# One more seven-product pair in each of the last two up-projection chunks

## The chip, the cores and the metric

The kernel runs on one core of a Trainium2 chip. The metric is the device time of one execution in microseconds (us); several executions are timed and their median is given. One further execution is recorded by the profiler, and it is from that one that all durations of single instructions come. The engines are TensorE (PE, with its weight loads as PEld), VectorE (DVE), ScalarE (ACT), GpSimd (POOL) and SyncE (SP). SP and POOL start almost all transfers; a transfer that adds to what lies at its destination (`accum_op`) is started from POOL here.

## The reference, cut to what matters

One decoder layer for 256 tokens of width 2048, in float32. The change lies in the last block, a feed-forward layer of width 8192:

```
D_MODEL = 2048; SEQ = 256; D_FF = 4 * D_MODEL

h    = _rmsnorm(x, norm_attn_pre)
proj = h @ w_in
...                                   # two kinds of attention, 8 heads each
x = x + _rmsnorm(mixed @ w_out, norm_attn_post)

h = _rmsnorm(x, norm_mlp_pre)
u = jnp.square(jax.nn.relu(h @ w_up))             # 256 x 2048 @ 2048 x 8192
x = x + _rmsnorm(u @ w_down, norm_mlp_post)       # 256 x 8192 @ 8192 x 2048
```

## The kernel before

**Products.** A float32 product is made of three TensorE passes: each operand is split into a high part (rounded by ACT, line 307 or 311) and a low part (the rest, by DVE, line 308 or 312), and the passes are high by high, high by low, low by high (`three`, and the loop at line 297). A pass takes 128 contraction rows, 128 tokens and 512 columns.

**The up projection.** `w_up` is worked on in eight chunks of 1024 columns (`NUP`, chunk index `j` from 0 to 7). A chunk's contraction has 16 blocks of 128 rows. `UP_STEPS[j]` lists a chunk's steps in the order in which they run:

- `("k", k)`: one block of 128 rows the plain way, two token halves by two column halves by three passes, so 12 matmuls.
- `("w", kp)` and `("p", kp)`: a pair, the blocks 2kp and 2kp+1 together, in Winograd's form of Strassen's method. The eight block products of the pair become seven, so 21 matmuls in place of 24 (`seven_products`). It needs four *left* sums of the activations `hT` (made once for each pair by `left_sums`, at the start of the phase) and sums `t` and `u` of the weights. In a `w` pair DVE makes `t` and `u` out of the two raw blocks (`seven`, lines 360 to 365). In a `p` pair they were made in HBM before, by transfers that add (`prepare`, `prepare_all`, tiles `sums`), and are loaded.

Before the change chunk 0 has no pairs. Chunks 1 to 5 have four, `p0`, `w1`, `p2`, `w3`, and eight plain blocks: 8 x 12 + 4 x 21 = 180 matmuls. Chunks 6 and 7 have three, `w0`, `w1`, `w2`, and ten plain blocks: 10 x 12 + 3 x 21 = 183.

The left sums of pairs 0 to 2 lie in tile `st` for the whole phase. Those of pair 3 lie in `st2`, which has the buffer that chunk 5's result `uT10` takes over; from then on they are gone.

**Partial results.** The seven products of a chunk's pairs add up in the chunk's four accumulators and in four more PSUM banks `m1`, `m5`, `m6`, `m7`. After the last pair, `close` puts these together into tile `c` (one ACT copy, line 1073, and four DVE operations, line 1076), and `up_evac` adds `c` to each accumulator (line 970), applies the rectifier and has the result transposed (`rt`) into `uT`.

**Order of the work.** The program order is written out by a small planner. `Flow` holds a clock that each matmul moves on by `MM` (0.2158 us, the planner's own figure); side jobs are generators that yield the time until their next step, and `flow.pump` issues those whose time has come. `Weights` runs ahead of TensorE: `get(i)` for a weight tile emits everything up to tile i+6 (`W_AHEAD`), which is the load into one of five `raw` buffers on SP (line 189) and the split into one of eight `hi`/`lo` pairs. Each engine works through its own instructions in program order, and so do SP and POOL with the transfers that they start: one that waits holds up those behind it.

**What `prepare` issues for one pair**, beginning at a planner time: two plain transfers on SP (lines 593 and 594: block 2kp into `t`, and the right half of block 2kp+1 twice into `u`), `D_PREP[2]` later three adds on POOL (lines 596 to 598, 256 KB each), and `D_PREP[2]` later one add of `t`'s left half to both halves of `u` (line 600, 512 KB). `prepare_all` begins at planner time 50 (`D_PREP[0]`) and goes through ten pairs, 24 us apart.

**How a pair's weights come in.** A `p` pair of chunks 1 to 4 loads `t` and `u` with one POOL transfer into tile `tu` (line 434), one of chunk 5 with two SP loads into `raw` (`j < 5` in the planning loop). A `w` pair loads its two blocks with POOL into tile `ab` (line 378), ahead of time; in chunk 7 the pairs `w1` and `w2` load theirs into two `raw` buffers instead (`raw_w`, in `seven_up`), at the place of their sums.

## Time and profile before

| | |
|---|---|
| median of 3 runs | 1049.08 us (1048.65 to 1049.19) |
| the profiled execution | 1049.02 us, of which its span is 1047.2 us |
| granted TensorE clock, mean | 0.998 |
| HBM read, written | 244.18 MB, 39.32 MB |

The span runs from the first to the last instruction that the profile shows; the 1.8 us beside it lie around it. TensorE's matmuls overlap, so the time that each is recorded with (about 0.39 us) is longer than the distance from one to the next. The chunks of the up projection can be told apart in the chain of work by the transposes `rt` of the chunk before, which stand at the beginning of each. A wait shown for an engine names what ended it.

### The profile page before, as it was taken

How to read it: one execution, taken by the hardware profiler on the slowest of the kernel's cores; microseconds unless marked ns; L12 is line 12 of the kernel's file. 1: busy time of each engine (PE TensorE's matmuls, PEld its weight loads, DVE VectorE, ACT ScalarE, POOL GpSimd, SP SyncE). 2: the span in 40 equal slices, each digit the busy share in tenths (PEclk: the TensorE clock that was granted, in tenths of full speed). 3: DMA queues.
4: the chain of work that ended last, by engine and by line, in shares of the span. 5: the costliest groups of instructions: out<-in, count | busy, mean ns of one | idle time of the engine just before them, and what ended most of it. 6: DMA issues, size and time to landing. Idle time of an engine off the chain costs nothing.

```text
span 1047.2 us, 13576 instructions
## 1 busy us (share of the span) xinstructions
PE 1036.6 (99%) x4844; PEld 863.3 (82%) x4844; DVE 809.0 (77%) x1080; ACT 633.5 (60%) x848; POOL 100.0 (10%) x157
## 2 busy tenths in 40 slices
PE   9999999999999999999999999999999999999996
PEld 6888889888888888888888888888888888888885
DVE  6676536567547669988889798887899988989995
ACT  6675536565545566766766666666567564766662
POOL 0011111112001010010100000000000001122100
PEclk9999999999999999999999999999999999999999
DMA  9999879699878295857766666469779767788952
GB/s 291 376 300 277 227 203 318 203 252 302 234 215 263 90 356 178 290 201 231 267 209 237 210 213 206 149 219 325 248 273 309 268 228 258 267 302 311 377 192 84
DMA packets 93140, 260.81 MB, mean 249 GB/s; under 512 B 8720, under 2 KB 12816, under 8 KB 91664
## 3 DMA queue, kind: packets, MB, share of 16 engines
q1 hardware_dynamic: 71056, 190.09, 52.6%
q0 software_dynamic: 21152, 68.69, 23.2%
q10 hardware_dynamic: 864, 1.16, 0.3%
q8 instruction: 38, 0.62, 0.2%
q14 instruction: 30, 0.25, 0.1%
HBM read 244.18 MB, written 39.32 MB: 271 GB/s over the span
## 4 chain that ended last, share of the span: by engine, by line
PE 97%; DVE 1%; DMA 1%; ACT 0%; issue 0%; POOL 0%; DVEq 0%; ACTq 0%
PE y L297 26%; PE acc_u L297 24%; PE acc_o L297 8%; PE m L297 7%; PE md L297 5%; PE acc_v L297 4%; PE acc_qk L297 4%; PE acc_ckv L297 2%; PE acc_q L297 2%; PE acc_ukv L297 2%; PE acc_cq L297 2%; PE acc_k L297 2%; PE acc_uq L297 2%; PE rt L301 1%; PE y L1221 1%; PE sc_b L297 1%
## 5 line engine op out<-in xcount | busy, mean ns | idle before, releaser
L308 DVE TENSOR_TENSOR lo<-raw,hi 128x1024 fp32r<-128x1024 f32 (+3 forms) x241 | 269.8, 1137 | 93.0 <-ACT hi L307 92.2
L307 ACT ACTIVATE hi<-raw 128x1024 fp32r<-128x1024 f32 (+3 forms) x241 | 234.8, 988 | 92.8 <-PE y L297 20.3
L297 PE MATMUL y<-hi,uhi 128*128 128x512 f32 x376 | 146.7, 390 | 0.0
L297 PE MATMUL y<-hi,ulo 128*128 128x512 f32 x376 | 146.4, 389 | 0.0
L297 PE MATMUL y<-lo,uhi 128*128 128x512 f32 x376 | 146.3, 389 | 0.0
L297 PE MATMUL acc_u<-hi,hT_hi 128*128 128x512 f32 x356 | 141.7, 398 | 0.0
L297 PE MATMUL acc_u<-hi,hT_lo 128*128 128x512 f32 x356 | 139.2, 391 | 0.4 <-DVE hT_lo L308 0.4
L297 PE MATMUL acc_u<-lo,hT_hi 128*128 128x512 f32 x356 | 138.8, 390 | 0.0
L312 DVE SCALAR_TENSOR_TENSOR lo<-raw,gcol,hi 128x1024 fp32r<-128x1024 f32 x72 | 90.7, 1280 | 15.9 <-ACT hi L311 15.6
L311 ACT ACTIVATE hi<-raw,gcol 128x1024 fp32r<-128x1024 f32 x72 | 81.7, 1149 | 19.1 <-DMA raw<-in_w_up 11.9
L297 PEld LDWEIGHTS y<-hi,ulo 128*128 128x128 f32 x376 | 70.6, 188 | 14.6
L297 PEld LDWEIGHTS y<-hi,uhi 128*128 128x128 f32 x376 | 70.6, 188 | 14.5
L297 PEld LDWEIGHTS y<-lo,uhi 128*128 128x128 f32 x376 | 70.6, 188 | 14.5
L297 PEld LDWEIGHTS acc_u<-hi,hT_lo 128*128 128x128 f32 x356 | 66.8, 188 | 15.0 <-DVE hT_lo L308 0.9
L297 PEld LDWEIGHTS acc_u<-lo,hT_hi 128*128 128x128 f32 x356 | 67.0, 188 | 13.0
L297 PEld LDWEIGHTS acc_u<-hi,hT_hi 128*128 128x128 f32 x356 | 66.9, 188 | 12.8
L297 PE MATMUL m<-hi,st 128*128 128x512 f32 x156 | 56.5, 389 | 0.0
L297 PE MATMUL acc_o<-hi,mixT_hi 128*128 128x512 f32 x128 | 51.8, 405 | 0.0
L308 DVE TENSOR_TENSOR lo<-st_down,hi 128x1024 fp32r<-128x1024 f32 x40 | 48.0, 1220 | 4.0 <-ACT hi L307 3.8
L297 PE MATMUL acc_o<-hi,mixT_lo 128*128 128x512 f32 x128 | 50.2, 392 | 0.0
L297 PE MATMUL acc_o<-lo,mixT_hi 128*128 128x512 f32 x128 | 50.0, 391 | 0.0
L307 ACT ACTIVATE hi<-st_down 128x1024 fp32r<-128x1024 f32 x40 | 42.1, 1052 | 11.1 <-PE y L297 9.5
(337 smaller groups left out, 2039.9 us busy)
## 6 DMA issues: line engine op xcount, KB each, us to landing
raw<-in_w_down SPq DMA_DIRECT2D x88, 512.0 KB, 6.2
raw<-in_w_up SPq DMA_DIRECT2D x86, 512.0 KB, 4.5
raw<-in_w_in SPq DMA_DIRECT2D x55, 512.0 KB, 6.7
raw<-in_w_out SPq DMA_DIRECT2D x32, 512.0 KB, 7.3
ab<-in_w_up POOLq DMA_DIRECT2D x28, 512.0 KB, 5.0
sums<-in_w_up SPq DMA_DIRECT2D x20, 512.0 KB, 6.9
ab_down<-in_w_down POOLq DMA_DIRECT2D x20, 512.0 KB, 6.5
tu<-sums POOLq DMA_DIRECT2D x8, 1024.0 KB, 5.2
```

Of the source, the lines that this page charges most:

```text
L297: nc.tensor.matmul(out, a, b, start=start, stop=stop)
L301: nc.tensor.transpose(out, a, ident)
L307: nc.scalar.activation(hi, src, AF.Copy)
L308: nc.vector.tensor_tensor(out=lo, in0=src, in1=hi.bitcast(F32), op=OP.subtract)
L311: nc.scalar.activation(hi, src, AF.Copy, scale=g)
L312: nc.vector.scalar_tensor_tensor(out=lo, in0=src, scalar=g, in1=hi.bitcast(F32), op0=OP.mult, op1=OP.subtract)
L1221: nc.tensor.matmul(out, a[x], w[z], start=False, stop=(x, z) == (1, 0), skip_group_check=True)
```

## The change

Chunks 6 and 7 get the step list of chunks 1 to 5: `p0`, `w1`, `p2`, `w3` and eight plain blocks in place of `w0`, `w1`, `w2` and ten plain blocks. What goes with it:

- `PREP` has fourteen pairs where it had ten. `prepare_all` goes through the first twelve, at 22.6 us apart with 11.3 us between the steps where it was 24 and 12.
- The last two, both of chunk 7, are prepared by two runs of `prepare` with `slow` = 10.0, started in chunk 2 and in chunk 4: the same bytes, with the last add cut into two, one transfer every 10 us, seven for a pair.
- `left_sums` writes pair 3's left sums to HBM (`st_kept`, 512 KB on SP) 8 us after it has made them. In chunks 6 and 7, at the fourth step, they are loaded into the buffer of tile `c`, which then lies idle until `close`; before `close` a new `c` is taken from that buffer, which is free once the last pair's products have been read.
- The `p` pairs of chunks 6 and 7 load their sums as those of chunk 5 do, by SP into `raw`. In chunk 7 no pair uses `ab` any more.
- The pause between `up_evac`'s add and its rectifier is 2.4 us where it was 1.8 in chunk 1.

```diff
 UP_STEPS = {0: [("k", k) for k in range(KD)]}
-for _j in range(1, 6):
+for _j in range(1, NUP):
     UP_STEPS[_j] = steps_of("k8 k9 k10 k11 p0 k12 w1 k13 p2 w3 k14 k15")
-for _j in range(6, NUP):
-    UP_STEPS[_j] = steps_of("k6 k7 k8 k9 k10 w0 k11 k12 w1 k13 w2 k14 k15")
...
-D_PREP = (50.0, 24.0, 12.0)
+D_PREP = (50.0, 22.6, 11.3)
...
-                ts, after = plan_seven(*seven_up(j, k), after, soon=j < NUP - 1 or k == 0)
+                ts, after = plan_seven(*seven_up(j, k), after, soon=j < NUP - 1)
...
-    def prepare(j, kp):
+    def prepare(j, kp, slow=0):
...
+        def add(out, src):
+            nc.gpsimd.dma_start(out=out, in_=src, accum_op=OP.add)
+
         nc.sync.dma_start(out=t, in_=a)
+        if slow:
+            yield slow
         nc.sync.dma_start(out=u.rearrange("p (k n) -> p k n", k=2), in_=twice(b[:, H:]))
-        yield D_PREP[2]
-        nc.gpsimd.dma_start(out=t[:, :H], in_=a[:, H:], accum_op=OP.add)
-        nc.gpsimd.dma_start(out=t[:, H:], in_=b[:, H:], accum_op=OP.add)
-        nc.gpsimd.dma_start(out=u[:, H:], in_=b[:, :H], accum_op=OP.add)
-        yield D_PREP[2]
-        nc.gpsimd.dma_start(out=u.rearrange("p (k n) -> p k n", k=2), in_=twice(t[:, :H]), accum_op=OP.add)
+        yield slow or D_PREP[2]
+        for out, src in ((t[:, :H], a[:, H:]), (t[:, H:], b[:, H:]), (u[:, H:], b[:, :H])):
+            add(out, src)
+            if slow:
+                yield slow
+        if not slow:
+            yield D_PREP[2]
+            add(u.rearrange("p (k n) -> p k n", k=2), twice(t[:, :H]))
+            return
+        for k in range(2):
+            add(u[:, k * H:(k + 1) * H], t[:, :H])
+            yield slow
...
-        for jk in PREP:
+        for jk in PREP[:-2]:
...
-            yield 1.8 if j < 10 else 2.4
+            yield 1.8 if 4 <= j < 10 else 2.4
...
+    st_kept = dram.tile([P, CW], F32, name="st_kept")
+
+    def new_c(name, dt=F32):
+        return late["up"].tile([P, 2 * CW], dt, tag="c", bufs=1, name=name)
...
+        if kp == 3:
+            yield 8.0
+            nc.sync.dma_start(out=st_kept, in_=sp.bitcast(F32))
...
+            if (j, t, b) in ((2, 2, 0), (4, 2, 0)):
+                flow.start(prepare(*PREP[j // 2 - 3], 10.0))
+            if j > 5 and (t, b) == (3, 0):
+                late["st2"] = new_c(f"st2_{j}", F32R)
+                nc.sync.dma_start(out=late["st2"][:, :CW].bitcast(F32), in_=st_kept)
+                sums[3] = parts_of(late["st2"])
...
             if last:
+                if j > 5:
+                    late["c"] = new_c(f"c_{j}")
                 more = close(closing(), m)
```

More of the change, by code (lines that the diff above doesn't have):

```diff
@@ L1024, in layer, with parts_of @@
     sums = []
+    st_kept = dram.tile([P, CW], F32, name="st_kept")
+    def new_c(name, dt=F32):
+        return late["up"].tile([P, 2 * CW], dt, tag="c", bufs=1, name=name)
+    def parts_of(st):
+        return [[st[:, w * 512 + i * P:w * 512 + (i + 1) * P] for w in range(2)] for i in range(4)]
     def left_sums(kp):
@@ L1101, in layer @@
                 late["st"] = late["up"].tile([P, 3 * CW], F32R, tag="st", bufs=1, name="st")
-                for n in ("ab", "c"):
-                    late[n] = late["up"].tile([P, 2 * CW], F32, name=n)
+                late["ab"], late["c"] = late["up"].tile([P, 2 * CW], F32, name="ab"), new_c("c")
                 late["st2"] = late["up"].tile([P, CW], F32R, tag="uT10", bufs=1, name="st2")
```

## The prediction

> **What bounds the kernel now.** I read the page first, then TensorE's waits, then the chain of waits in order of time.
>
> ```profile
> span 1047.2 us, 13576 instructions
> PE 1036.6 (99%) x4844; PEld 863.3 (82%) x4844; DVE 809.0 (77%) x1080; ACT 633.5 (60%) x848; POOL 100.0 (10%) x157
> ```
> ```profile
> PE warm L538 <- DVE zero L535: 1.2, 1, 1.2
> PE acc_qk L297 <- ACT hi L307: 0.8, 1, 0.8
> PE acc_u L297 <- DVE hT_lo L308: 0.4, 1, 0.4
> PE qrt L301 <- DVE qT L805: 0.2, 1, 0.2
> ```
>
> TensorE is the bound from end to end. Its waits for other engines come to 2.6 us, none of them in chunks 1 to 7. So there is no stall to remove: the change gains what it takes out of TensorE's stream, and loses whatever stalls it makes.
>
> What is a matmul worth? The chain shows stretches that nothing interrupts, and the first full stretch behind the first transposes of each chunk:
>
> ```profile
> 482.28 8.16 PE acc_u L297 x36
> ...
> 533.59 2.09 PE acc_u L297 x9
> ...
> 576.32 2.09 PE acc_u L297 x9
> ...
> 619.80 2.08 PE acc_u L297 x9
> ...
> 663.24 2.10 PE acc_u L297 x9
> ...
> 706.64 2.08 PE y L297 x9
> ```
>
> 36 matmuls in 8.16 us are 0.2267 us each. From 533.59 to 576.32, chunk 4 with its 180 matmuls takes 42.73 us. From 619.80 to 663.24, chunk 6 takes 43.44 us, and from 663.24 to 706.64 chunk 7 takes 43.40 us, with 183 matmuls and the same sixteen transposes.
>
> **The change part by part.**
>
> *The products.* In each of chunks 6 and 7, two plain blocks (24 matmuls) become one pair (21). That is 6 matmuls fewer, 6 x 0.2267 = 1.36 us. The chunks say the same in another way: (43.44 - 42.73) + (43.40 - 42.73) = 1.38 us. I take **-1.4 us**, all of it on the path, since TensorE waits for nothing there.
>
> *DVE in chunks 6 and 7.* Two `w` pairs take the place of three, so DVE makes one set of sums fewer and has two plain blocks fewer to split, against one pair more to split. DVE is off the path; I count nothing.
>
> *Twelve early pairs in place of ten.* Pairs 1 to 10 move up by 1.4 us each. Pairs 11 and 12 (of chunk 6) are new; worked out from the delays and the planner's 0.216 us a matmul, they fall into the output projection, about 300 to 350 us.
>
> ```profile
> sums<-in_w_up SPq DMA_DIRECT2D x20, 512.0 KB, 6.9
> sums<-in_w_up POOLq DMA_DIRECT2D x30, 256.0 KB, 8.9
> sums<-sums POOLq DMA_DIRECT2D x10, 512.0 KB, 9.2
> ```
> ```profile
> 300.00:350.00 50.00, 50.00 (x222) 41.06 (x221) 29.63 (x41) 24.38 (x40) 3.37 (x3) 1.00 0.71 231
> ```
>
> A pair is two plain transfers, three small adds and one large one, 2.25 MB written. Two pairs are 4.5 MB, at this window's 231 GB/s 19.5 us of transfers, against 0.29 x 50 = 14.5 us in which the transfer engines stand idle there, and a TensorE that is busy for 50.00 of 50 us. The cost lies between 0 and the 5 us that do not fit; I take 0, because weights are made several tiles ahead and a delay first eats that lead. POOL matters as well, since it computes the norms' powers that the next phase waits for:
>
> ```profile
> 321.80 1.20 POOL L600 DMA_DIRECT2D sums<-sums  x1
> 349.10 0.56 POOL L518 TENSOR_TENSOR rstd_post<-t_post,neg_half 128x1 f32<-128x1 f32 x1 [26.10 <-DVE t_post L517]
> 362.42 0.55 POOL L518 TENSOR_TENSOR rstd_post<-t_post,neg_half 128x1 f32<-128x1 f32 x1 [12.76 <-DVE t_post L517]
> ```
>
> Pair 12's small adds come some 4 us of planner time ahead of the first `rstd_post`, so they should go out near 330 us and have landed before 349. Its last add stands between the two `rstd_post`: it goes out at about 350 and takes 1.2 us of POOL, with 12.76 us to spare. Cost 0. If the small adds slip behind the first `rstd_post`, the last one waits 8.9 us for them and still ends at about 362.
>
> *Two pairs by small transfers in chunks 2 to 5.* Seven transfers each, 10 us of planner time apart, two on SP and five on POOL. POOL has `tu` and `ab` loads there that wait long for DVE, and the adds queue among them:
>
> ```profile
> 459.52 0.54 POOL L378 DMA_DIRECT2D ab<-in_w_up  x1 [3.05 <-DVE lo L308]
> 470.07 0.54 POOL L434 DMA_DIRECT2D tu<-sums  x1 [10.01 <-DVE lo L308]
> 494.83 0.54 POOL L434 DMA_DIRECT2D tu<-sums  x1 [22.48 <-DVE lo L308]
> ```
>
> By the planner's times the first add falls between these first two rows, the second before the third row, and so on: nearly all fall into POOL's gaps of 10 and 22 us and cost it about 1 us of issue each. One can push an `ab` load back by 1 us. I take 0, that load's lead being several us.
>
> The Trainium skill (DMA: Bandwidth & Descriptors, "Rules for kernel authors") advises the opposite, to coalesce small transfers into large ones. The rows bear this out for the single transfer: 256 KB of adds land in 8.9 us, 512 KB in 9.2 us, so cutting the last add in two buys a second landing. Going by the rule, a pair here costs one landing more; the sum stays the same, since these sums are needed only in chunk 7.
>
> *Pair 3's left sums, out.* `st_kept` goes on SP 8 us of planner time after its sums are made. SP runs ahead of DVE, so it will wait there, with a `raw` load behind it:
>
> ```profile
> 403.47 0.33 SPq L189 DMA_DIRECT2D raw<-in_w_up  x1
> ```
> ```profile
> 417.09 0.68 DVE L1042 TENSOR_TENSOR st<-c,st 128x512 fp32r<-128x512 f32 x1
> 422.90 1.82 DVE L308 TENSOR_TENSOR lo<-raw,hi 128x512 fp32r<-128x512 f32 x2
> 427.22 2.35 DVE L308 TENSOR_TENSOR lo<-tu,hi 128x1024 fp32r<-128x1024 f32 x2
> ```
> ```profile
> 420.83 1.57 ACT L307 ACTIVATE hi<-raw 128x512 fp32r<-128x512 f32 x2
> ```
> ```profile
> 431.82 0.68 PE m L297 x3
> ```
>
> By the planner's times `st_kept` comes just ahead of the load at 403.47. `st` is complete only at 417.09 + 0.68 = 417.8, so that load moves from 403.5 to about 418.3, and its split on ACT, the second of the two at 420.83 (from 421.35), is next. Loads of this stretch and of the whole run land as follows:
>
> ```profile
> DMA to landing us min/median/max: 3.5/4.5/5.5
> ```
> ```profile
> DMA to landing us min/median/max: 2.7/5.5/15.9
> ```
>
> At 4.5 us it lands at 422.8, 1.4 us late for ACT; DVE, which has about 1.1 us of room there, is 0.4 us late. At 15.9 us it lands at 434.2, and DVE is 11.8 us late. The smallest lead behind it is that of the first `tu` tile: ready at 428.4, used at 431.8 (the row of `m`), 3.4 us. So the cost to TensorE is between 0 and 8.4 us, with 0 up to a landing of 7.5 us. I take 0, by the nearest row, the stretch's own largest of 5.5 us.
>
> *Pair 3's left sums, back.* `c` carries them from the fourth step to the last pair, and `close` must wait until the last pair's products are read.
>
> ```profile
> L1073 ACT ACTIVATE c<-m x7: 575/577/581, 440.0 to 697.0; 128x512 f32<-128x512 f32 x7
> ```
>
> It does so already: in chunk 1 the pairs' last matmul begins near 439 and the copy at 440.0. What is queued behind it on ACT are splits for the next chunk. Cost 0. Two loads of 512 KB on SP wait for the `c` of the chunk before, which is read by then. The longer pause in chunk 1 delays transposes, not TensorE: 0.
>
> *Loads in chunk 7.* Five `raw` buffers serve 8 plain blocks, 2 x 4 loads of `p` and 2 x 2 of `w`, 20 loads, where there were 10 + 4. In a `p` beside a `w`, `u` takes the buffer of five loads before. DVE then has 0.69 + 1.23 us of splits and four sums to do meanwhile:
>
> ```profile
> 680.60 0.68 DVE L363 TENSOR_TENSOR t<-raw_w 128x512 f32<-128x512 f32 x1
> ...
> 682.52 0.69 DVE L365 TENSOR_TENSOR u<-u,raw_w 128x512 f32<-128x512 f32 x1
> ...
> 688.53 1.22 DVE L308 TENSOR_TENSOR lo<-t,hi 128x1024 fp32r<-128x1024 f32 x1
> ```
> ```profile
> 696.00 1.36 PE m L297 x6
> ```
> ```profile
> DMA to landing us min/median/max: 3.5/4.4/7.8
> ```
>
> The sums run from 680.60 to 683.2, so about 4.5 us lie between. A load needs 4.4 us and ACT's split 1.05 (the `raw` splits above): 1 us of idle DVE, twice in the chunk. At 7.8 us it is 4.4 us, twice. The last `w` tile is ready at 689.75 and used at 696.00, a lead of 6.2 us. So 0 by the median, up to 2.6 us by the maximum; I take 0. In chunk 6 the loads are those of chunk 5, which stalls nowhere.
>
> **Sum.** 1047.2 - 1.4 = 1045.8 us of span; with the 1.8 us around it 1047.6. The profiled execution (1049.02) lies 0.06 us below the median of the runs, so **1047.7 us**.
>
> **The rivals.**
>
> 1. *SP stands behind `st_kept`.* For it: 14 us of blocked SP in the stretch with the smallest leads. Against: 0 cost up to a landing of 7.5 us. At 9.2 us, the largest adding transfer's median, DVE is 5.1 us late and TensorE 1.7 us: 1049.4 us, the gain just gone.
> 2. *Chunk 7 starves for `raw` buffers, and the kernel is slower.* It decides once 2 x (landing - 3.4) passes 6.2, a landing of 6.5 us. With the 9.2 us of the adding transfers TensorE loses 11.6 - 6.2 = 5.4 us: 1053.1 us. Against: the 4.4 us median.
> 3. *A matmul is worth what it is recorded with.*
>
> ```profile
> L297 PE MATMUL m<-hi,st 128*128 128x512 f32 x156 | 56.5, 389 | 0.0
> ```
>
> 6 x 0.389 = 2.3 us would give 1046.7. Against: 36 in 8.16 us.
>
> 4. *The transfers share one pool.* The row of 300:350 leaves up to 5 us that do not fit; if half of it gets through to TensorE, 1047.7 + 2.5 = 1050.2 us. The Trainium skill (DMA: Bandwidth & Descriptors, "Issuing engines are not separate DMA queues") says that transfers from all queues run on the same sixteen engines and interleave, so moving work to POOL would spare SP's loads nothing; no row here separates the two.
>
> **How the numbers follow.** Forecast 0.70, within 1047.3 to 1048.1. Rival 1: 0.11. Rival 2: 0.07. Rival 3: 0.03. Rival 4: 0.09. About 0.2% (2.1 us) is what a measurement of this kernel can tell from no change; the forecast lies within it. Faster is rival 3, 0.03. Slower is rival 2 and the far end of rivals 1 and 4: 0.07 + 0.02 = 0.09. The rest, 0.88, is the same. The range reaches from 1047.0 to 1049.6, over the forecast and rival 1, and leaves out rivals 2, 3 and 4, 0.19.
>
> **What would show it.** Chunks 6 and 7 at 42.7 us each in the chain. TensorE's waits still without a row in chunks 1 to 7. SP's load behind `st_kept` at 418, ACT idle about 1 us for it near 421.4. A wait of PE for `lo` near 432 or in chunk 7 is rival 1 or 2; one for `hi` or `hT_lo` before 380 is rival 4. A chunk that gets shorter by more than 0.7 us would make the worth of a matmul wrong.

## The result: slower by 0.8%, and the profile after

The changed kernel takes 1057.65 us (median of 6 runs, 1054.79 to 1060.76) against 1049.13 us before, a ratio of 1.008 with a 95% interval of 1.0066 to 1.0093. The profiled execution is the shortest of the six, 1054.79 us with a span of 1053.0 us, 5.8 us more than before.

From the page of the changed kernel: its span, and busy time with its share of the span and number of instructions for each engine.

```profile
span 1053.0 us, 13632 instructions
...
PE 1037.0 (98%) x4838; PEld 861.8 (82%) x4838; DVE 808.2 (77%) x1078; ACT 636.9 (60%) x852; POOL 113.9 (11%) x171
```

TensorE's waits in the changed kernel (what it waited for: us in total, times, longest):

```profile
PE rt L299 <- ACT r L983: 2.1, 4, 0.7
PE acc_u L295 <- DVE c L1095: 1.7, 2, 1.4
PE acc_u L295 <- ACT hT_hi L305: 1.7, 1, 1.7
...
PE m L295 <- DVE lo L306: 0.8, 1, 0.8
```

The six matmuls are gone (4844 recorded before, 4838 now). Four waits of the up projection that the kernel before did not have are there in their place. Where they fall is seen by cutting the up projection at the first transposes `rt` of each chunk. Starts of instructions, worked out from each trace, in us; "chunk 0" runs from the last `w_out` matmul to the transposes that stand at the start of chunk 1, "rest" from the transposes behind chunk 7 to the end. Differences in the text are taken before rounding:

| kernel | before chunk 0 | chunk 0 | 1 | 2 | 3 to 5 | 6 | 7 | rest | span |
|---|---|---|---|---|---|---|---|---|---|
| before | 354.5 | 49.4 | 43.6 | 42.8 | 128.9 | 43.4 | 43.5 | 341.2 | 1047.2 |
| changed | 353.9 | 51.5 | 48.3 | 42.1 | 128.9 | 42.7 | 44.2 | 341.6 | 1053.0 |
| changed, second profile | 354.2 | 51.2 | 48.3 | 42.1 | 128.9 | 42.7 | 44.6 | 341.6 | 1053.6 |

So the time went to three places: **chunk 0** (+2.0 us), **chunk 1** (+4.7, of which chunk 2 gives 0.7 back, so +4.0 together), and **chunk 7**, which should have shortened by 0.7 like chunk 6 and is 0.7 longer. Chunk 6 has its gain. The second profile, of a run described below, has the same three places.

**Chunk 0.** The changed kernel's timeline on POOL, on SP's queue and on ScalarE (start, duration, engine, line, operation; in brackets how long the engine sat idle before it, and what ended that):

```profile
338.84 3.02 POOL L592 DMA_DIRECT2D sums<-in_w_up  x3
348.48 0.57 POOL L516 TENSOR_TENSOR rstd_post<-t_post,neg_half 128x1 f32<-128x1 f32 x1 [6.62 <-DVE t_post L515]
353.42 1.20 POOL L592 DMA_DIRECT2D sums<-sums  x1 [4.37 <-issue]
361.82 0.57 POOL L516 TENSOR_TENSOR rstd_post<-t_post,neg_half 128x1 f32<-128x1 f32 x1 [7.20 <-DVE t_post L515]
```
```profile
355.83 0.38 SPq L187 DMA_DIRECT2D raw<-in_w_up  x1
```
```profile
364.37 1.15 ACT L309 ACTIVATE hi<-raw,gcol 128x1024 fp32r<-128x1024 f32 x1 [3.89 <-DMA raw<-in_w_up]
...
366.80 1.07 ACT L305 ACTIVATE hT_hi<-ht 128x512 fp32r<-128x512 f32 x2
```

POOL runs in the order that the prediction gave: pair 12's three small adds ahead of the first `rstd_post`, its last add between the two, both `rstd_post` on time. The times are later than forecast: the small adds go out at 338.8 in place of about 330, the last add at 353.4 in place of 350. What is late is a transfer of another queue: the raw `w_up` load that SP issues at 355.83, beside that last add. And ScalarE works in order: while it waits 3.89 us for this load (1.00 us in the kernel before), `hT_hi`, for which TensorE waits, stands behind the split.

**Chunk 1.** The chain of waits of the changed kernel, in order of time (start, us, what held the chain):

```profile
421.21 8.99 DMA ab<-in_w_up
...
430.32 1.24 DVE t L358
...
440.51 4.46 DMA raw<-in_w_up
...
445.07 1.16 ACT hi L309
...
452.84 0.70 ACT r L983
453.58 0.66 PE rt L299 x4
```

On DVE, the first load that SP had held back, and then that `ab` load:

```profile
425.72 1.23 DVE L306 TENSOR_TENSOR lo<-raw,hi 128x1024 fp32r<-128x1024 f32 x1 [0.74 <-ACT hi L305]
430.32 1.23 DVE L358 TENSOR_TENSOR t<-ab 128x1024 f32<-128x1024 f32 x1 [3.38 <-DMA ab<-in_w_up]
```

The first link is again a transfer, the second of POOL's two `ab` loads for pair `w3`, at 9.0 us. In the kernel before, the same two loads (issued between 418 and 421 us; KB each, median us from issue to landing) took 4.0:

```profile
ab<-in_w_up POOLq DMA_DIRECT2D x2, 512.0 KB, 4.0
```

DVE waits 3.38 us for it, makes `w3`'s sums late, frees the `raw` buffers late, a load that waits for a buffer lands late, and the copy `c<-m` of `close`, with all that follows from it, is late.

**Chunk 7.** SP's queue and ScalarE in the changed kernel:

```profile
657.52 1.67 SPq L187 DMA_DIRECT2D raw_w<-in_w_up  x2
662.71 0.33 SPq L187 DMA_DIRECT2D raw<-sums  x1
```
```profile
668.34 1.06 ACT L305 ACTIVATE hi<-raw 128x1024 fp32r<-128x1024 f32 x1 [3.19 <-DMA raw<-sums]
...
669.79 0.68 ACT L983 ACTIVATE r<-acc_u,rstd_pre 128x512 f32<-128x512 f32 x1
```

Two of the five `raw` buffers hold `w1`'s raw blocks ahead of time, the second load of `p0`'s sums (the first goes out at 656.3) finds a buffer only at 662.7, and again it is ScalarE's order that carries it to TensorE: `r`, which the transposes need, stands behind the split. TensorE waits 0.6 us for it here, and another 0.7 us for `r` at the end of the chunk.

### The profile page after: what moved, and what is told of

The parts are those of the page before. It is cut to its first block, busy times and chain, and to the rows that moved or that the text cites. A ratio compares the mean times of both kernels' runs of the same rounds, so it can differ in the third digit from the quotient of the medians.

```text
span 1053.0 us, 13632 instructions
## 1 busy us (share of the span) xinstructions
PE 1037.0 (98%) x4838; PEld 861.8 (82%) x4838; DVE 808.2 (77%) x1078; ACT 636.9 (60%) x852; POOL 113.9 (11%) x171
## 4 chain that ended last, share of the span: by engine, by line
PE 85%; issue 6%; DMA 4%; DVE 3%; ACT 1%; POOL 0%; DVEq 0%; ACTq 0%; POOLq 0%
PE y L295 25%; PE acc_u L295 14%; PE acc_o L295 8%; PE m L295 5%; PE md L295 5%; PE acc_v L295 4%; PE acc_qk L295 4%; PE acc_ckv L295 2%; PE acc_ukv L295 2%; PE acc_q L295 2%; PE acc_cq L295 2%; PE acc_k L295 2%; PE acc_uq L295 2%; DVE lo L306 2%; DMA raw<-in_w_up 1%
## 5 line engine op out<-in xcount | busy, mean ns | idle before, releaser
L306 DVE TENSOR_TENSOR lo<-raw,hi 128x1024 fp32r<-128x1024 f32 (+3 forms) x253 | 282.6, 1133 | 102.6 <-ACT hi L305 101.6
L305 ACT ACTIVATE hi<-raw 128x1024 fp32r<-128x1024 f32 (+3 forms) x253 | 245.9, 985 | 116.5 <-DMA raw<-in_w_in 26.0
L295 PE MATMUL acc_u<-hi,hT_hi 128*128 128x512 f32 x344 | 137.3, 399 | 3.3 <-DVE c L1095 1.7
L295 PE MATMUL acc_u<-hi,hT_lo 128*128 128x512 f32 x344 | 134.5, 391 | 0.5 <-DVE hT_lo L306 0.5
L295 PE MATMUL acc_u<-lo,hT_hi 128*128 128x512 f32 x344 | 134.0, 390 | 0.0
L295 PEld LDWEIGHTS acc_u<-hi,hT_hi 128*128 128x128 f32 x344 | 64.6, 188 | 16.6 <-DVE c L1095 2.5
L295 PEld LDWEIGHTS acc_u<-hi,hT_lo 128*128 128x128 f32 x344 | 64.6, 188 | 14.8 <-DVE hT_lo L306 0.9
L295 PEld LDWEIGHTS acc_u<-lo,hT_hi 128*128 128x128 f32 x344 | 64.7, 188 | 12.3
L295 PE MATMUL m<-hi,st 128*128 128x512 f32 x168 | 60.8, 389 | 0.0
L305 ACT ACTIVATE hi<-st_down 128x1024 fp32r<-128x1024 f32 x40 | 42.1, 1053 | 11.3 <-PE y L295 9.8
```

Source lines behind the costliest of these rows:

```text
L295: nc.tensor.matmul(out, a, b, start=start, stop=stop)
L305: nc.scalar.activation(hi, src, AF.Copy)
L306: nc.vector.tensor_tensor(out=lo, in0=src, in1=hi.bitcast(F32), op=OP.subtract)
```

## The experiments

The theory is those three places, named **A** (pair 12's last add beside chunk 0's raw load), **B** (SP blocked by `st_kept`; the loads held back go out together and slow the `ab` loads) and **C** (chunk 7's `raw` buffers). All edits below are against the changed kernel or, where it says so, the kernel before. What each run measured stands in one table at the end of this section.

**The changed kernel again.**

> The changed kernel once more, for a second profile of it. If the three losses read from its first profile are what it always has, the stretch around chunk 0 is again about 2 us longer than before, that of chunk 1 about 4 us and that of chunk 7 about 1.5 us; what a slower execution (up to 1060.8) has on top should show as further waits of TensorE in the opening or in chunks 0 and 1.

It had 1055.41 us (1051.99 to 1059.33), and the stretches shown above as the second profile: the three places are not of one execution.

**A, undone.** Pair 12 is taken out of the opening and prepared by a third slow run:

```diff
-        for jk in PREP[:-2]:
+        for jk in PREP[:-3]:
...
-            if (j, t, b) in ((2, 2, 0), (4, 2, 0)):
-                flow.start(prepare(*PREP[j // 2 - 3], 10.0))
+            if j in (2, 3, 4) and (t, b) == (2, 0):
+                flow.start(prepare(*PREP[j - 5], 10.0))
```

> The changed kernel with the twelfth early pair taken out of the opening: it is prepared by small transfers in chunks 2 to 4, and chunk 7's two pairs begin in chunks 3 and 4. Theory: the twelfth pair's last adding transfer (issued at 353.4, landed at 360.6) made the weight load issued at 355.8 land at 364.4, 8.6 us instead of 5.7; ACT stood 3.9 us for it ahead of the splits of hT, and TensorE lost 2.0 us in chunk 0. Then the time from the last w_out matmul to chunk 0's first transpose (49.4 us before, 51.4 with the change) comes back to 49.4 and the span falls by 2.0 to about 1051. Rival: POOL's order (the norm's power behind the adds) is what is late; then the wait for hT stays in part, because pair 11 still has its adds there.

Chunk 0 is back at 49.5 us. What lies before chunk 0 took until 356.3 us in this profile, 2.4 longer, so the span hardly moved and missed the 1051 us expected.

**A, alone.** The kernel before, with the two pairs of chunk 6 prepared in the opening at the change's pace, their sums unused:

```diff
-D_PREP = (50.0, 24.0, 12.0)
+D_PREP = (50.0, 22.6, 11.3)
+MORE = [(6, 0), (6, 2)]
...
-        for jk in PREP:
+        for jk in PREP + MORE:
```

> The kernel before, with the eleventh and twelfth pair prepared in the opening at the change's pace (22.6/11.3) and nothing else; their sums are not used. Theory A (the twelfth pair's last adds beside chunk 0's raw load): the stretch from the opening's end to chunk 0's first transposes goes from 49.4 to 51 to 52.5 us, with the scalar engine idle for that raw load near 360 to 364; time 1050.5 to 1053, and a spread between executions of 3 us or more, as in the changed kernel. Rival (the loss needs the rest of the change): 49.4 and 1049.2.

And the same without pair 12's last add (`if (j, kp) != (6, 2)` ahead of it):

> As the run with the two further pairs alone in the kernel before, but without pair 12's last add (512 KB, out about 353 us), whose sums are not used. Theory (that one transfer, beside the raw load of about 356, is what the opening loses): from the opening's end to chunk 0's first transposes 49.4 to 49.8 us where it was 52.9, the raw load lands within 6 us, the time 1049 to 1050. Rival (pair 12's small adds and the rest of its traffic do it as well): 51 us or more, 1051 or more.

Groups of transfers between 353 and 366 us (KB each, median us from issue to landing), with the last add and without it:

```profile
sums<-sums POOLq DMA_DIRECT2D x1, 512.0 KB, 9.8
raw<-in_w_up SPq DMA_DIRECT2D x1, 512.0 KB, 8.6
```
```profile
raw<-in_w_up SPq DMA_DIRECT2D x1, 512.0 KB, 5.7
```

One transfer of 512 KB on POOL's queue makes SP's raw load land in 8.6 us in place of 5.7. Chunk 0 goes from 49.4 to 52.8 us with it (a little past what was expected) and is 49.5 without it. In place, A is shown: it is that add, not the twelfth pair's bytes as a whole. In time the second run missed its expectation by a little: 1050.33 us, with an interval that holds no change (0.9997 to 1.0016); chunk 1 was 1.1 us longer in its profile, and 1.0 us in that of the run with the add, so that part is not the last add's.

**A, by placing.** Pair 12 stays in the opening at a pace of 21.4/10.7 (and B and C are undone as shown further down), so that its last add goes out earlier:

```diff
-D_PREP = (50.0, 22.6, 11.3)
+D_PREP = (50.0, 21.4, 10.7)
```

> Pair 12 back in the opening, but at a pace of 21.4/10.7 us instead of 22.6/11.3, so that its last add goes out about 14 us earlier in the order of work than in the changed kernel, ahead of the last half of the opening, and not beside the raw w_up load that is issued near 356; the write of pair 3's left sums a tile later and chunk 7's loads a tile later as in the run before; the two slow pairs in chunks 2 and 4 as in the change. Theory A (pair 12's last add slows that raw load, and the scalar engine's splits queue behind it): the opening's end to chunk 0's first transposes comes back to 49.4 us from 51.4, the raw load lands within 6 us of its issue, and the time is 1048.0 to 1050. Rival (twelve pairs are too many for the opening wherever they stand): 51 or more, or w_out ends later than 356.5; time 1051 or more.

Chunk 0 49.4 us, the raw load at 5.6 us, 1048.85 us. The last add now goes out at 338.0 in place of 353.4, and the same bytes cost nothing there that chunk 0 or the opening shows.

**B, undone.** The write of pair 3's left sums a good deal later, when SP no longer overtakes DVE's sums:

```diff
-            yield 8.0
+            yield 40.0
             nc.sync.dma_start(out=st_kept, in_=sp.bitcast(F32))
```

> The changed kernel with one number altered: pair 3's left sums are written to HBM 40 us of planner time after they are made instead of 8, so that SP no longer stands waiting for them in chunk 1. Theory: in chunk 1 SP stood 14 us behind that transfer and then let it and the held-back weight loads go together with POOL's two ab loads, which landed at 427.6 and 430.2 instead of 422.6 and 423.9; DVE stood idle 3.4 us for the second and TensorE lost about 4 us between chunk 1's first transpose and chunk 2's. Then that stretch (43.6 us before, 48.3 us with the change) comes back to about 44.2 us and the profiled span falls from 1053.0 to about 1049. Rival: the longer pause before chunk 1's rectifier, or the 512 KB themselves, cost the time; then the stretch stays near 48 us.

Chunk 1 comes down from 48.3 to 44.3 us. The span, 1051.0, is 2 us over the expected one; chunk 0 took 52.5 us in this profile. With A undone as well:

> Both of the two other alterations together. If the two losses are separate, they add: chunk 0 as before, chunk 1 about 0.6 us longer than before, and what is left of the change is 6 matmuls fewer (1.4 us) against the waits at the ends of chunks 6 and 7 (about 1.9 us): a span near 1047.5, a time near 1049.3, and the wide spread of the single times gone. If the losses feed each other, one of the two alterations gives most of it and the sum falls short.

Both places are back (49.4 and 44.0), but the time is 1051.97 us, not 1049.3, and the spread (4 us) is not gone: C remains, and the opening ended at 356.5 us in this profile.

**B, alone.** The kernel before, with the write and nothing that reads it:

```diff
+        if kp == 3:
+            yield 8.0
+            nc.sync.dma_start(out=st_kept, in_=sp.bitcast(F32))
```

> The kernel before, with the write of pair 3's left sums to HBM added at the change's place (8.0) and nothing else; what is written is not read. Theory B (the blocked SP queue and its burst are what chunk 1 lost, whatever the pairs do): the stretch of chunk 1 goes from 43.56 to 46.5 to 48.5 us, the time from 1049.1 to 1052 to 1054. Rival (it takes the extra slow transfers or the twelfth pair as well): 43.5 to 44.5 us and 1049 to 1050.

It is 1053.13 us, a ratio of 1.0039 (1.0026 to 1.0052), with 4.0 us in chunk 1. The write alone thus costs nearly three times what the products bring. Is it the 512 KB or the wait? The same, with two columns (1 KB) in place of all:

```diff
-            nc.sync.dma_start(out=st_kept, in_=sp.bitcast(F32))
+            nc.sync.dma_start(out=st_kept[:, :2], in_=sp[:, CW - 2:].bitcast(F32))
```

> The kernel before, with a write at the same place and with the same wait as in the run of the write alone, but of two columns of the left sums (1 KB) in place of all 1024 (512 KB). SP is blocked as long; only the bytes are gone. Theory (SP's loads, held back and let go together, slow the ab loads): the stretch of chunk 1 stays at 46.5 to 47.6 us, the time at 1052 to 1053. Rival (the 512 KB written beside them are what takes the time): 43.5 to 44.5 us, 1049 to 1050. In between, both have a part.

Transfers between 418 and 432 us (total, then groups with KB each and median us to landing) in the kernel before, with the whole write, and with 1 KB:

```profile
DMA packets 871, 3.24 MB, mean 231 GB/s; under 512 B 98, under 2 KB 98, under 8 KB 855
...
ab<-in_w_up POOLq DMA_DIRECT2D x4, 512.0 KB, 4.9
raw<-in_w_up SPq DMA_DIRECT2D x3, 512.0 KB, 4.5
```
```profile
DMA packets 1297, 4.73 MB, mean 338 GB/s; under 512 B 144, under 2 KB 144, under 8 KB 1296
...
raw<-in_w_up SPq DMA_DIRECT2D x6, 512.0 KB, 7.3
ab<-in_w_up POOLq DMA_DIRECT2D x2, 512.0 KB, 8.2
st_kept<-st SPq DMA_DIRECT2D x1, 512.0 KB, 3.0
```
```profile
DMA packets 1297, 4.20 MB, mean 300 GB/s; under 512 B 272, under 2 KB 272, under 8 KB 1296
...
raw<-in_w_up SPq DMA_DIRECT2D x6, 512.0 KB, 6.4
ab<-in_w_up POOLq DMA_DIRECT2D x2, 512.0 KB, 6.5
```

With 1 KB, SP stands as long and six raw loads fall into the window in place of three; chunk 1 is 46.9 us. `w3`'s second `ab` load took 4.1 us in the kernel before, 7.7 with 1 KB and 8.9 with the whole write; chunks 1 and 2 together are longer by 3.3 and 4.0 us. So most of the 4.0 us is there without the write's bytes. The 0.7 between the two runs is of one profile each, and their times (ratios 1.0039 and 1.0026) do not tell them apart.

Does it matter which loads are held back? The write at 13 in place of 8 has one more load ahead of it (A undone here):

> As the run with both parts undone (pair 12 late, the write of the left sums late), but that write's place set between the change's and the late one: 13 instead of 8 or 40. The load that stood right behind the write in the change now stands ahead of it; the write still blocks SP until pair 3's sums are done, near 418, and loads behind it go out together. Theory (the loads that were held back go out in a burst and slow the ab loads on POOL's queue, and pair 0's left sums of chunk 1 come late): chunk 1 stays long, 46 to 48.5 us from its first transposes to those of chunk 2 (44.0 with the write late), with the ab transfers at 7 us or more; time 1054 to 1056. Rival (only the load right behind the write counted): 44 to 45 us, time 1052.

Chunk 1 stays at 48.2 us; the profile is of the slowest of four executions. The one load that stood right behind the write, on which the prediction had looked, is not what costs.

**C.** To the run with A and B undone, chunk 7's sums and raw blocks of the pairs are planned one tile ahead in place of `SUMS_AHEAD`:

```diff
-        at = max(len(weights.specs) - SUMS_AHEAD, after)
+        at = max(len(weights.specs) - ahead, after)
...
-                ts, after = plan_seven(*seven_up(j, k), after, soon=j < NUP - 1)
+                ts, after = plan_seven(*seven_up(j, k), after, soon=j < NUP - 1, ahead=SUMS_AHEAD if j < NUP - 1 else 1)
```

> Compared with the kernel that has both alterations (late left sums, pair 12 in the chunks). One thing altered: in chunk 7 a w pair's sums, and with them its two raw_w loads, come one weight tile later in the program, behind the load of the p pair's last tile in the case of w1 and behind the load of u in the case of w3. Theory: at the start of chunk 7 two of the five raw buffers were taken by raw_w ahead of p0's t, whose load had to wait for a buffer until 662.7 and landed at 668.2; ACT stood 3.2 us for it with the rectifier r behind it, and the transposes came late. With t loaded first, ACT does not stand there: the stretch from chunk 7's first transpose to that of the down projection, 44.7 us, falls to 43.5 or less, TensorE's waits for r (1.9 us) to under 1, and the time by about 1 us. Rival: it is the load of the left sums that holds up SP; then the stretch stays at 44.7.

SP's queue and ScalarE in that run:

```profile
652.59 1.52 SPq L187 DMA_DIRECT2D raw<-sums  x2
655.29 4.01 SPq L187 DMA_DIRECT2D raw_w<-in_w_up  x2
```
```profile
660.72 0.69 ACT L983 ACTIVATE r<-acc_u,rstd_pre 128x512 f32<-128x512 f32 x1
661.31 1.05 ACT L305 ACTIVATE hi<-raw 128x1024 fp32r<-128x1024 f32 x1
```

Both loads of `p0`'s sums now go out ahead of `w1`'s raw blocks, their splits are over before the transposes that begin at 663.5, `r` stands behind no late load, the wait at the chunk's beginning is gone, and chunk 7 is 43.5 us where it was 44.7 (43.4 and 43.8 in the two further runs with this edit). But the run with A undone, which has the change's own order in chunk 7, was at 43.5 us as well: there `p0`'s second load landed in 4.9 us, ScalarE sat idle 2.58 us for it, and TensorE did not wait. In the six other profiles with that order the load took 5.5 to 5.9 us and chunk 7 44.2 to 45.3. So the place of the wait is shown; what it costs hangs on that load's landing, execution by execution. The rest of C, 0.8 us over chunk 6, is at its end, where TensorE waits 0.9 us for `r`; no run tried to take that away. The rival for chunk 7 was that SP stood behind the load of `st2`; that load was moved two steps on in chunk 7, with A and B undone:

```diff
-            if j > 5 and (t, b) == (3, 0):
+            if j > 5 and (t, b) == (2 * j - 9, 0):
```

> Compared with the same kernel. One thing altered: in chunk 7 the left sums are fetched at the sixth step instead of the fourth, so that SP meets that transfer, which waits for DVE's last add into the chunk before, later. Rival theory of chunk 7: SP stood behind that transfer (issued at 667.4, right after the last add at 666.7 to 667.3), with weight loads behind it; then the 44.7 us fall to about 43.5. Theory of the raw buffers: the load that ACT stood for was issued at 662.7, ahead of that transfer, so nothing changes: 44.7 us, within 0.4.

Chunk 7 is 45.3 us, no shorter (a little over the 0.4 us that the theory allowed): this rival falls.

**The slow pairs.** In some runs with three slow pairs, or with other work moved beside them, chunks that had stalled nowhere in the changed kernel have a wait at their end. In the run at 21.4/10.7 it was chunk 2's (43.4 us). Its timeline on POOL, then on ScalarE:

```profile
471.57 0.53 POOL L376 DMA_DIRECT2D ab<-in_w_up  x1 [0.60 <-DVE lo L306]
472.09 0.91 POOL L592 DMA_DIRECT2D sums<-in_w_up  x1
```
```profile
482.39 1.15 ACT L309 ACTIVATE hi<-raw,gcol 128x1024 fp32r<-128x1024 f32 x1 [3.32 <-DMA raw<-in_w_up]
483.45 0.58 ACT L1092 ACTIVATE c<-m 128x512 f32<-128x512 f32 x1
```

One add of 256 KB, right behind an `ab` load, and the raw load at the chunk's end is late for ScalarE with `c<-m` behind it. Can it be placed away? The first slow pair at 20.6 us a step:

```diff
-                flow.start(prepare(*PREP[j // 2 - 3], 10.0))
+                flow.start(prepare(*PREP[j // 2 - 3], 20.6 if j == 2 else 10.0))
```

> As the run at a pace of 21.4/10.7, with the first slow pair (started in chunk 2) at 20.6 us a step in place of 10. There one of its adds went out on POOL right behind an ab load, at 472.1 us, and the first raw load of the end of that chunk took 6.6 us and the scalar engine stood 3.3 us for it; by the planner's times the adds now stand behind the tu loads instead. Theory (an add counts by which load it lies beside): the wait of 1.5 us before chunk 2's transposes goes, chunk 1's end to chunk 2's from 43.4 to 42.1 to 42.3 us, span 1046.0 to 1046.5, time 1047.3 to 1048.0. Rival (it moves to another chunk's end): span 1047 or more and 1048.5 to 1049.5.

The same places in that run:

```profile
559.21 1.76 POOL L592 DMA_DIRECT2D sums<-in_w_up  x2
560.32 1.49 POOL L592 DMA_DIRECT2D sums<-sums  x1
```
```profile
569.75 1.15 ACT L309 ACTIVATE hi<-raw,gcol 128x1024 fp32r<-128x1024 f32 x1 [3.65 <-DMA raw<-in_w_up]
570.81 0.58 ACT L1092 ACTIVATE c<-m 128x512 f32<-128x512 f32 x1
```

Chunk 2 is 42.1 us, as the theory said, but three adds now meet ahead of chunk 4's end, and the same wait stands there. The rival holds, and the time, 1052.77 us, is worse than either theory gave. That an add beside an `ab` load does it is not shown, though. In the changed kernel, too, an add goes out on POOL right behind an `ab` load in chunk 2, at 477.8 us, and is still under way when the raw load is issued at 481.8; that load lands in 4.0 us, and ScalarE sits idle 0.72 us ahead of `c<-m`. The two runs with the pair in chunk 6 alone, below, have such an add in chunk 2 as well and lose nothing there. So the slow pairs lie near loads without slack and some executions lose 1.3 to 2.3 us there; what decides it is open.

**What the products bring.** The pair in chunk 6 alone, with chunk 7 as before the change, the write late, ten early pairs at the old pace and chunk 6's two pairs slow; then the same with the ten early pairs at 22.6/11.3:

```diff
-for _j in range(1, NUP):
+for _j in range(1, NUP - 1):
     UP_STEPS[_j] = steps_of("k8 k9 k10 k11 p0 k12 w1 k13 p2 w3 k14 k15")
+UP_STEPS[NUP - 1] = steps_of("k6 k7 k8 k9 k10 w0 k11 k12 w1 k13 w2 k14 k15")
```

> Only chunk 6 gets the fourth pair; chunk 7 keeps its list of before (three pairs, w0 through ab). Ten early pairs at 24 us as before, chunk 6's two pairs by small transfers in chunks 2 to 5, the left sums written 40 us late. Theory: chunk 7's waits came from twenty loads through five raw buffers, two of them held by raw_w loaded ahead, so ACT stood for a load of sums with the rectifier behind it; without them nothing is lost and the gain is that of three matmuls, 0.7 us: span about 1046.5, time about 1048.4. Rival: the load of the left sums on SP at the fourth step of a chunk, which waits for DVE's last adds, holds up the loads behind it; then chunk 6 loses time here too, and the total is 1049.5 or more.

> The kernel with the fourth pair in chunk 6 alone (1048.39 us), with the ten early pairs at the change's pace of 22.6 and 11.3 us in place of 24 and 12. It asks where the changed kernel's spread (1054.8 to 1060.8) and the 2 us come from that two of the altered kernels lost before the last w_out matmul (356.3 and 356.5 us against 354.5 before and 353.9 in the changed kernel's profile). Theory: the denser pace makes the transfers of the opening collide with weight loads and attention work, differently from run to run; then this one is 1 to 3 us slower than 1048.4 with a spread of 3 us or more. Rival: the opening varies by itself, whatever the pace; then it is 1048.4 within 0.7.

1048.39 and 1048.65 us: the size of half the gain, no new wait in their up projections, and no loss to the pace that the times show, so the theory given for the second run falls; both intervals still hold 1. Chunk 6 is 42.7 us in every run that has the pair. Then the version that the runs point to: chunk 6 alone, all twelve pairs in the opening at 21.4/10.7, no slow pairs, the write late, the pause of 1.8 us again.

> The version that the runs point to: the further pair in chunk 6 alone (chunk 7 as before the change), all twelve pairs in the opening at 21.4/10.7, no slow pairs, the write of the left sums late, the pause in chunk 1 at 1.8 again. Theory (nothing is left that takes more than it gives): chunk 0's stretch 49.4, chunk 1 43.6 to 44.2, chunk 6 42.7, chunk 7 43.4; span 1046.3 to 1046.9, time 1047.7 to 1048.6, a ratio of 0.9985 to 0.9993. Rival (twelve pairs in the opening cost something even at this pace): chunk 0 or w_out longer, time 1049 or more.

1049.22 us against 1049.79 beside it: no difference to be seen, where 1047.7 to 1048.6 and a ratio of at most 0.9993 were expected. A wait of 0.7 us before chunk 1's transposes was left. The change's longer pause there, alone in the kernel before:

```diff
-            yield 1.8 if j < 10 else 2.4
+            yield 1.8 if 4 <= j < 10 else 2.4
```

> The kernel before with the change's pause (2.4 in place of 1.8 between up_evac's add and its rectifier in chunk 1) and nothing else. All variants with the write made late had 44.0 to 44.3 us in chunk 1, against 43.56 before. Theory (the pause is that half microsecond): 44.0 to 44.2 us, time 1049.6. Rival (it costs nothing, and the half microsecond is of the extra transfers): 43.5 to 43.7 us, time 1049.1 to 1049.4.

Chunk 1 is 44.0 us as the theory said, but it is no loss: chunk 2 is 42.1 in place of 42.8, and the time, 1048.74 us, is below what either side expected (ratio 0.9985 to 1.0003). The pause moves the transposes by which the two are told apart; together they are 86.1 us against 86.4. (So B's own part of the changed kernel's chunk 1 is the +4.0 us given above.) With the pause, the version becomes:

> The version with the further pair in chunk 6 alone and twelve early pairs, with the longer pause in chunk 1 as well, which alone took 0.25 us off chunks 1 and 2 together (86.36 to 86.1) and did away with the wait before chunk 1's transposes. Theory (small gains add): chunks 1 and 2 together 86.0 to 86.2, chunk 6 42.7, span 1046.0 to 1046.5, a ratio of 0.998 to 0.9993. Rival (the opening's own changes from execution to execution cover a gain of this size): span 1046.5 or more, or a ratio whose interval holds 1.

TensorE's waits in it:

```profile
PE warm L537 <- DVE zero L534: 1.2, 1, 1.2
PE acc_u L296 <- DVE hT_lo L307: 0.4, 1, 0.4
PE acc_qk L296 <- ACT hi L306: 0.2, 1, 0.2
PE qrt L300 <- DVE qT L815: 0.2, 1, 0.2
```

The up projection has no wait left that the kernel before had not. 1048.01 us against 1049.14 beside it, a ratio of 0.9989 (0.998 to 0.9998): the one version whose interval lies below the kernel before, if narrowly. It is one of several versions tried, and the pause alone had a span of 1046.1 against its 1046.0, so the times do not show how much of it is the pair's; that chunk 6 is 0.7 us shorter, the profiles do.

All runs, with the ratio to the kernel before on the same chip:

| run | chunk 0 | 1 | 2 | 3 to 5 | 6 | 7 | span | median us (range, runs) | ratio, 95% |
|---|---|---|---|---|---|---|---|---|---|
| e0_again | 51.2 | 48.3 | 42.1 | 128.9 | 42.7 | 44.6 | 1053.6 | 1055.41 (1051.99-1059.33, 5) | 1.0036-1.0081 |
| e1_late_kept | 52.5 | 44.3 | 42.3 | 128.9 | 42.7 | 44.7 | 1051.0 | 1053.32 (1048.66-1055.43, 7) | 1.0015-1.0052 |
| e2_pair12_late | 49.5 | 47.7 | 42.1 | 129.1 | 42.7 | 43.5 | 1052.5 | 1054.37 (1053.44-1055.05, 4) | 1.0033-1.0063 |
| e3_both | 49.4 | 44.0 | 42.0 | 129.2 | 42.7 | 44.7 | 1050.2 | 1051.97 (1050.28-1054.29, 9) | 1.0017-1.0037 |
| e4_chunk6_only | 49.5 | 44.1 | 42.0 | 128.9 | 42.7 | 43.4 | 1047.2 | 1048.39 (1047.18-1050.18, 10) | 0.9983-1.0002 |
| e5_sums_later | 49.4 | 44.2 | 42.1 | 130.6 | 42.7 | 43.5 | 1048.7 | 1050.58 (1049.36-1052.56, 10) | 1.0006-1.0024 |
| e6_st2_later | 49.4 | 44.1 | 42.0 | 130.4 | 42.7 | 45.3 | 1050.7 | 1051.46 (1048.78-1053.72, 10) | 1.0009-1.0028 |
| e7_pace | 49.4 | 44.2 | 42.1 | 128.8 | 42.7 | 43.4 | 1046.9 | 1048.65 (1047.03-1050.78, 11) | 0.9982-1.0 |
| e8_pace21 | 49.4 | 44.2 | 43.4 | 128.9 | 42.7 | 43.4 | 1047.5 | 1048.85 (1048.02-1052.88, 10) | 0.9987-1.0008 |
| e9_kept13 | 49.5 | 48.2 | 42.1 | 130.0 | 42.7 | 45.1 | 1056.5 | 1055.39 (1053.82-1058.33, 4) | 1.0044-1.0081 |
| e10_kept_alone | 49.4 | 47.6 | 42.8 | 128.9 | 43.5 | 43.4 | 1051.3 | 1053.13 (1052.03-1053.95, 5) | 1.0026-1.0052 |
| e11_twelve_alone | 52.8 | 44.5 | 42.8 | 128.9 | 43.5 | 43.5 | 1051.0 | 1052.48 (1050.56-1054.87, 6) | 1.0013-1.0042 |
| e12_kept_tiny | 49.4 | 46.9 | 42.8 | 128.9 | 43.4 | 43.4 | 1050.7 | 1052.33 (1051.07-1053.17, 7) | 1.0015-1.0036 |
| e13_no_last_add | 49.5 | 44.6 | 42.8 | 128.9 | 43.4 | 43.4 | 1047.6 | 1050.33 (1048.23-1051.39, 10) | 0.9997-1.0016 |
| e14_slow_apart | 49.5 | 45.1 | 42.1 | 131.2 | 42.7 | 43.8 | 1049.8 | 1052.77 (1049.63-1055.26, 8) | 1.0021-1.0043 |
| e15_six_early | 49.4 | 44.3 | 42.8 | 128.9 | 42.7 | 43.4 | 1046.8 | 1049.22 (1048.12-1052.55, 12) | 0.9990-1.0007 |
| e16_pause | 49.4 | 44.0 | 42.1 | 128.9 | 43.5 | 43.5 | 1046.1 | 1048.74 (1047.68-1049.79, 10) | 0.9985-1.0003 |
| e17_six_pause | 49.4 | 44.0 | 42.1 | 128.9 | 42.7 | 43.4 | 1046.0 | 1048.01 (1047.06-1049.32, 11) | 0.9980-0.9998 |

## Why the prediction was wrong

The forecast was 1047.7 us and no difference; the kernel is 0.8% slower. Half the gain was found as forecast, and three costs taken at nothing were not nothing.

- **The products** (-1.4 us): right for chunk 6, which is 42.7 us in every run with the pair, 0.7 less. Chunk 7 was never under 43.4 us with its pair, what it took before, so that half of the gain was not seen in any run.
- **Twelve early pairs, "Cost 0"**: the first failed step. The prediction had summed the bytes of a window of 50 us and had weighed POOL's issue order; the order came out as said, with the last add 3.4 us later. It did not look at which loads of the other queue lie beside the last add. That add alone takes 3.4 us of chunk 0 in the kernel before (52.8 against 49.4; 49.5 without the add) and 2.0 in the changed one. Rival 4, "the transfers share one pool", had the mechanism, at a chance of 0.09. The page that it named, the Trainium skill's DMA: Bandwidth & Descriptors ("Issuing engines are not separate DMA queues"), agrees with the trace here: moving work to POOL's queue did not spare SP's load, 8.6 us against 5.7. The wait that this rival was to be known by, before 380, was for `hi` or `hT_lo`; the one that came was for `hT_hi`. That the rival's size (2.5 us) is near is luck: it was half of what did not fit into 300 to 350 us, and the loss is one collision behind that window.
- **Pair 3's left sums, out, "0"**: the second. The step followed the one load behind the blocked write: it landed in time, DVE stood 0.74 us for it, much as said. Missed were the further loads that wait behind it on SP and go out at once, and that POOL's `ab` loads, issued within two microseconds of it, then take 7.6 and 9.0 us. Rival 1 had the place, and its sign, a wait of TensorE for `lo`, came with 0.8 us, but it looked for the price on that load (1.7 us); it is 4.0 us, and the write alone shows it.
- **Loads in chunk 7, "I take 0"**: the third. `p0`'s second load does wait for a buffer, as rival 2 had it, but not where it was sought: TensorE waited for no weights there, and the wait came through ScalarE's queue to the transposes. In the changed kernel's first profile chunk 7 is 1.5 us longer than chunk 6; 0.6 us of it is this wait, and 0.7 us stands at the chunk's end, whose cause no run tested.
- **The slow pairs, "0"**: true of the changed kernel's two profiles (chunks 2 to 5 show no wait); that it held there is luck in part, since some other runs lost 1.3 to 2.3 us in those chunks, and no run tells what decides it.
- **`c` and the pause, "0"**: right; with the pause alone, chunks 1 and 2 are even 0.3 us shorter in its profile. The two loads into `c` have no run of their own beyond the one that moved chunk 7's.

One omission is common to these. The prediction asked of each late load how much lead the *weights* had on TensorE, several us. But ScalarE works in order, and behind the split of a late load stand instructions with next to no lead: `hT_hi` in chunk 0, `c<-m` at each chunk's end, `r` for the transposes. The kernel before already shows it, in chunk 1 on ScalarE, just ahead of `c<-m`:

```profile
438.97 1.15 ACT L311 ACTIVATE hi<-raw,gcol 128x1024 fp32r<-128x1024 f32 x1 [2.20 <-DMA raw<-in_w_up]
```

2.20 us of idle time there cost TensorE nothing, nor did 2.95 us in chunk 1 of the run with the late write alone; at 3.2 to 3.9 us, in the rows shown above, TensorE waited.

The three places and the gain account for the profiled execution: -0.6 (opening) + 2.0 + 4.0 (chunks 1 and 2) - 0.7 + 0.7 + 0.4 (rest) = 5.8 us, which is all of it. They do not account for the median, which is 2.9 us higher still. By medians the kernel before with A alone is 3.2 us slower and with B alone 3.8, against 8.5 us for the changed kernel, and 6.3 when it was run again. Part of the spread lies before the up projection: the opening ended between 353.6 and 357.4 us over all profiles, and in the three longest ones TensorE waited 1.4 to 3.1 us for the attention's `s_a`. Such a wait (0.2 us and more) stands in seven of the eleven profiles at the pace 22.6/11.3 and in none of the nine at 24/12 or 21.4/10.7, between 50 and 200 us, long before pair 12. That points at the pace as a further cost; but four profiles at that pace are without it, and the run that tested the pace showed no loss in its time. What sets it in an execution stays open.

## What to carry to other kernels

Price a moved transfer by the loads that it lies beside, not by the mean load of a window, and follow each late load through the in-order queue of the engine that takes it, to the instruction with the least lead. A transfer that waits on a queue holds back the loads behind it, and when they then go out together, they slow those of other queues; issue it where its source is surely complete. And where everything fits but for a single collision, moving that one transfer (here by 15 us) can be worth as much as the arithmetic that was saved.

## What the runs showed of the hardware

An add from HBM to HBM can cost its neighbours more than its share of the bytes. Busy share of the transfer engines in tenths, and what they moved, in 40 slices between 353 and 366 us: the run with the two pairs but without pair 12's last add (a store of `x` and the raw load, alone), then the run with that add.

```profile
DMA  0000000009999992939099970000000000000000
GB/s 0 0 0 0 0 0 0 0 0 378 403 403 403 429 378 50 378 76 328 38 391 441 429 303 13 0 0 0 0 0 0 0 0 0 0 0 0 0 0 0
```
```profile
DMA  1000000000999989293999984999999960000000
GB/s 25 0 0 0 0 0 0 0 0 6 183 347 353 328 302 429 76 504 57 447 227 290 258 233 76 271 302 302 302 302 302 296 246 13 0 0 0 0 0 0
```

Without the add 1.57 MB go within about 16 slices, 5.2 us; with it 2.11 MB, a third more, take about 25, 8.1 us. Slices that are 90% busy or more move 328 to 441 GB/s without the add, and many of them 227 to 302 GB/s with it. The raw load lands in 8.6 us in place of 5.7, the store in 6.6 in place of 4.8. In the changed kernel's first profile the add's packets even ran alone for 2.6 us, at 50 to 132 GB/s, before the store and the load began; here they did not, and the raw load is as late. So the busy share of a window, and its mean rate, from which the prediction had worked out room for two pairs, say little of what an add leaves to others.
